# Sparse attention on one core: attention values with the values as the stationary operand, probabilities scaled before they are transposed, three branches added up in PSUM

## The chip, the cores and the metric

The kernel runs on one core of one Trainium2 chip. The metric is the device time of one execution in microseconds (us); the numbers below are medians of several runs, and the trace is one further execution, taken by the hardware profiler. The engines are called as the profile calls them: PE (TensorE, with PEld for its weight loads), DVE (VectorE), ACT (ScalarE), POOL (GpSimd) and SP (SyncE, which issues most DMAs).

## The reference

The program is a stack of thirteen residual layers on 256 tokens of width 1024: seven feed-forward layers, a gated recurrence, a forgetting attention, a short convolution, shared keys and values, and last a sparse attention followed by one more feed-forward layer. The change is in the sparse attention alone. With 16 heads in 4 groups, 256 tokens and every 64-token block selected, it is

```python
p_c = masked_softmax(s_c, rel_c >= 0)                      # 15 compressed keys
o_c = jnp.einsum('bghqn,bgnd->bghqd', p_c, v_c)
p_s = masked_softmax(s_s, (rel_s >= 0)[:, :, None])        # selected blocks
o_s = jnp.einsum('bghqk,bgqkd->bghqd', p_s, v_sel)
p_w = masked_softmax(s_w, mask_w)                          # window
o_w = jnp.einsum('bghqk,bgkd->bghqd', p_w, v_wb)
return gblk[..., 0:1] * o_c + gblk[..., 1:2] * o_s + gblk[..., 2:3] * o_w
...
return out @ w_o
```

## The kernel before

Everything stays on the core; the weights stream in from HBM, 1 MB at a time. A weight piece is split by ACT into a high part `wh` (L177) and by DVE or POOL into a low part `wl` (L179), and each product of the big layers is three matmuls of a 128x128 stationary tile with 256 columns. The order on every engine is the order in which the code emits instructions; there is no scheduler. `tick()` may emit one such split at the points where it is called, paced by a running cost `self.t`. Inside the sparse attention all low parts go to POOL (`pool_parts`).

The sparse attention (`nsa`) works on eight pairs of heads, c = 0 to 7, one after the other. Queries are in halves: token tile 0 sees 128 keys (`p0`), token tile 1 sees 256 (`p1`), each for two branches `br` (selected, window) and two heads `h`. One turn of the loop, in emission order:

- `probs(c)`: PE transposes the twelve 128x128 tiles of p (L250), ACT and DVE copy them out to `pT`, DVE makes r = gate / sum (L1224, L1226).
- `outputs(c - 1)`: PE transposes the finished output `oc` of the pair before (two tiles), ACT rounds it to `zh`, DVE makes the rest `zl`.
- `scores(c + 1)`: PE makes the scores of the next pair, `kT<-qT`, with the two heads on the two halves of TensorE's rows; DVE adds the bias and takes the row minimum (L1191, L1201), ACT takes the exponential and the row sum (L1193, L1203, each followed by the read of the accumulator).
- `values(c)`: twelve products with `pT` stationary and 64 columns of `vv` moving, then eight DVE instructions that scale by r and add into `oc` (L1248). `cmp_values` has put the compressed branch into `oc` beforehand.
- `fill(n)`: n pieces of other work for PE, twelve matmuls each: the later query projections, then the output projection of the pairs already done, each piece followed by one DVE addition into x.

`p1` and `p0` have one buffer each: the reduce for pair c + 1 overwrites the tiles that `probs(c)` has transposed. The value products use one PSUM bank (`O`), scores and transposes share five (`R`).

Of the kernel before, what the change touches and what calls it, by code (L numbers as in the profile page):

```python
# [8 lines left out]
F32 = mybir.dt.float32  # L9
# [4 lines left out]
ALU = mybir.AluOpType  # L14
# [104 lines left out]
class Builder:  # L119
# [979 lines left out]
    def nsa(self, nxt):  # L1099
        nc, tc = self.nc, self.tc  # L1100
        xs = self.xs
        P, B = self.P, self.comp(self.P)
        A, R, O = P[:2], B + [P[2]], P[3:]
        self.ring_at[tuple(P)] = 2
        with tc.tile_pool(name="nsa", bufs=1, reuse_waits="tile") as pl:
            qT = pl.tile([128, 8, 256], F32, name="qT", tag="qT")
            pc = pl.tile([128, 2, 8, 32], F32, name="pc", tag="pc")
            pcT = pl.tile([128, 2, 256], F32, name="pcT", tag="pcT")
            oc = pl.tile([128, 8, 2, 128], F32, name="oc", tag="oc")
            gt = pl.tile([128, 2, 48], F32, name="gt", tag="gt")  # L1110
            qg = pl.tile([128, 1], F32, name="qg", tag="qg")
            nc.gpsimd.memset(pc, 0.0)
# [1 line left out]
            bts, ps, pTs, zs, qs, late = {}, {}, {}, {}, [], []  # L1114
# [50 lines left out]
                    nc.scalar.copy(pcT[:, j], b[:, 0:256])  # L1165
                self.tick()

            def cmp_values(gp):
                for j in range(2):
                    b = self.bank(R)  # L1170
                    for i in range(2):
                        self.mm(b[:, 256 * i:256 * i + 256], pcT[:, j, 128 * i:128 * i + 128], self.vcz[:, gp], cost=432.0)
                    c = 4 * gp + 2 * j
                    nc.scalar.copy(oc[:, c:c + 2].rearrange("p c i d -> p i c d"), b.rearrange("p (i c d) -> p i c d", i=2, c=2))
                self.tick()

            def scores(c):

                gp, bt = c // 4, bts[c]
                p1 = pl.tile([128, 2, 2, 256], F32, name="p1", tag="p1")  # L1180
                p0 = pl.tile([128, 2, 2, 128], F32, name="p0", tag="p0")
                mx = pl.tile([128, 2, 2, 2], F32, name="mx", tag="mx", bufs=2)
                sm = pl.tile([128, 2, 2, 2], F32, name="sm", tag="sm", bufs=2)

                rows = [slice(64 * h, 64 * h + 64) for h in range(2)]
                s1 = [self.bank(R), self.bank(R)]
                for h in range(2):
                    self.mm(s1[h], qT[rows[h], c, 128:256], self.kT[rows[h], gp].rearrange("p r s -> p (r s)"), cost=429.0)
                for h in range(2):
                    for br in range(2):  # L1190
                        nc.vector.tensor_tensor_reduce(  # L1191
                            p1[:, br, h], s1[h][:, 256 * br:256 * br + 256], bt[:, h], 1.0, 3e38, ALU.add, ALU.min, mx[:, 1, br, h:h + 1])
                        nc.scalar.activation(  # L1193
                            p1[:, br, h], p1[:, br, h], AF.Exp, bias=mx[:, 1, br, h:h + 1], scale=-1.0, accum_out=sm[:, 1, br, h:h + 1])
                    self.tick()
                s0 = [self.bank(R), self.bank(R)]
                for h in range(2):
                    self.mm(s0[h][:, 0:256], qT[rows[h], c, 0:128], self.kT[rows[h], gp, :, 0:128], cost=216.0)
                for h in range(2):
                    for br in range(2):  # L1200
                        nc.vector.tensor_tensor_reduce(  # L1201
                            p0[:, br, h], s0[h][:, 128 * br:128 * br + 128], bt[:, h, 128:256], 1.0, 3e38, ALU.add, ALU.min, mx[:, 0, br, h:h + 1])
                        nc.scalar.activation(  # L1203
                            p0[:, br, h], p0[:, br, h], AF.Exp, bias=mx[:, 0, br, h:h + 1], scale=-1.0, accum_out=sm[:, 0, br, h:h + 1])
                self.tick()
                if c + 2 < 8:
                    bias(c + 2)
                ps[c] = (p1, p0, sm)

            def probs(c):  # L1210
                p1, p0, sm = ps.pop(c)
                r = pl.tile([128, 2, 2, 2], F32, name="r", tag="r", bufs=2)
                pT = pl.tile([128, 2, 2, 384], F32, name="pT", tag="pT")
                for br in range(2):
                    for h in range(2):
                        b = self.bank(R)
                        self.transpose(b[:, 128:256], p1[:, br, h, 0:128])
                        self.transpose(b[:, 256:384], p1[:, br, h, 128:256])
                        self.transpose(b[:, 0:128], p0[:, br, h])
                        if h:  # L1220
                            nc.vector.tensor_copy(pT[:, br, h], b[:, 0:384])
                        else:
                            nc.scalar.copy(pT[:, br, h], b[:, 0:384])
                nc.vector.reciprocal(r, sm)  # L1224
                gg = gt.rearrange("p i (h r) -> p i r h", r=3)[:, :, 1:3, 2 * c:2 * c + 2]
                nc.vector.tensor_tensor(r, r, gg, op=ALU.mult)  # L1226
                self.tick()
                pTs[c] = (pT, r)

            def values(c):  # L1230
                gp = c // 4
                pT, r = pTs.pop(c)
                o = self.bank(O)
                for i in range(2):
                    for br in range(2):
                        for h in range(2):
                            at = 256 * i + 128 * br + 64 * h
                            d = slice(64 * (2 * gp + h), 64 * (2 * gp + h) + 64)
                            for kt in range(i + 1):
                                s = pT[:, br, h, 128 * (i + kt):128 * (i + kt) + 128]  # L1240
                                self.mm(o[:, at:at + 64], s, self.vv[:, kt, br, d], kt == 0, kt == i, cost=214.0)
                        self.tick()
                for br in range(2):
                    for i in range(2):
                        for h in range(2):
                            at = 256 * i + 128 * br + 64 * h
                            on = oc[:, c, i, 64 * h:64 * h + 64]
                            nc.vector.scalar_tensor_tensor(on, o[:, at:at + 64], r[:, i, br, h:h + 1], on, op0=ALU.mult, op1=ALU.add)  # L1248

            def outputs(c):  # L1250
                if c % 2 == 0:
                    zs[c // 2] = (
                        pl.tile([128, 2, 256], F32R, name="zh", tag="zh", bufs=2),
                        pl.tile([128, 2, 256], F32R, name="zl", tag="zl", bufs=2),
                    )
                zh, zl = zs[c // 2]
                b = self.bank(O)
                for i in range(2):
                    self.transpose(b[:, 128 * i:128 * i + 128], oc[:, c, i])
                nc.scalar.copy(zh[:, c % 2], b[:, 0:256])  # L1260
                nc.vector.tensor_tensor(zl[:, c % 2], b[:, 0:256], zh[:, c % 2].bitcast(F32), op=ALU.subtract)

            def stream():

# [44 lines left out]
            def fill(n):  # L1309
                for _ in range(n):  # L1310
                    next(main, None)
# [4 lines left out]
            query(1)  # L1316
            cmp_scores(0)
            scores(0)
            fill(3)
            for c in range(8):  # L1320
                probs(c)
                if c:
                    outputs(c - 1)
                if c == 0:
                    g = self.nat_heads_in_two(pl, late[:1], ("qa",), pool=True)
                    q = next(g)
                if c % 4 == 0:
                    cmp_turn(c // 4)
                if c == 3:
                    query(2)  # L1330
                    query(3)
                if c < 7:
                    scores(c + 1)
                    if c == 3:
                        cmp_scores(1)
                    if c % 4 == 0:
                        cmp_values(c // 4)
                    if c == 1:
                        for _ in g:
                            pass  # L1340
                        qs += q
                    values(c)
                    fill((1, 0, 2, 2, 2, 2, 2)[c])
                    if c == 0:
                        for _ in g:
                            pass
                        qs += q
                    if c == 0:
                        g = self.nat_heads_in_two(pl, late[1:], ("qb",), pool=True)
                        q = next(g)  # L1350
            fill(1)
            values(7)
            fill(1)
            outputs(7)
            fill(4)
            self.P = B

    def run(self):
# [209 lines left out]
```

## Time and profile before

| what | value |
|---|---|
| median of 3 runs (lowest to highest) | 2142.56 us (2142.15 to 2143.3) |
| profiled execution: time / span from first to last instruction | 2140.52 us / 2138.4 us |
| mean granted TensorE clock of the profiled execution | 0.994 |
| busy share PE / DVE / ACT / POOL | 98% / 66% / 48% / 19% |
| the sparse attention's loop over pairs, in the trace | 1858.86 to 1944.2 us |

A busy time of PE counts pipelined matmuls whose ends are modelled, so 98% says that PE seldom stands still, not that it runs at its peak. The granted clock is 1.0 at the upper level (2.4 GHz) and 0.5 at the lower (1.2 GHz). The time of a run lies about 2 us above the span.

### The profile page before, as it was taken

How to read it: one execution, taken by the hardware profiler on the slowest of the kernel's cores; microseconds unless marked ns; L12 is line 12 of the kernel's file. 1: busy time of each engine (PE TensorE's matmuls, PEld its weight loads, DVE VectorE, ACT ScalarE, POOL GpSimd, SP SyncE). 2: the span in 40 equal slices, each digit the busy share in tenths (PEclk: the TensorE clock that was granted, in tenths of full speed). 3: DMA queues.
4: the chain of work that ended last, by engine and by line, in shares of the span. 5: the costliest groups of instructions: out<-in, count | busy, mean ns of one | idle time of the engine just before them, and what ended most of it. 6: DMA issues, size and time to landing. Idle time of an engine off the chain costs nothing.

```text
span 2138.4 us, 41531 instructions
## 1 busy us (share of the span) xinstructions
PE 2087.5 (98%) x17299; PEld 2064.0 (97%) x17299; DVE 1419.4 (66%) x2566; ACT 1027.9 (48%) x2076; POOL 401.4 (19%) x357
## 2 busy tenths in 40 slices
PE   8999889999999998999999999999999999999999
PEld 7999889999999998999999999999999999879999
DVE  7656776756666578575667657775578665687554
ACT  5544434544444456654454445454445444565442
POOL 2002646300100023320010001110021100442000
PEclk9999999999999999999999999999999999999999
DMA  7554423595455545345545554555546554223551
GB/s 264 199 191 149 158 80 122 181 238 196 152 205 190 175 158 183 133 175 200 178 158 207 188 179 156 200 193 181 186 174 228 179 185 170 97 101 131 211 190 60
DMA packets 57020, 368.93 MB, mean 173 GB/s; under 512 B 6318, under 2 KB 10694, under 8 KB 14080
## 3 DMA queue, kind: packets, MB, share of 16 engines
q1 hardware_dynamic: 53600, 355.49, 46.3%
q0 software_dynamic: 2656, 10.07, 2.5%
q8 instruction: 135, 2.21, 0.4%
q10 hardware_dynamic: 576, 0.72, 0.1%
q14 instruction: 53, 0.43, 0.1%
HBM read 360.75 MB, written 4.46 MB: 171 GB/s over the span
## 4 chain that ended last, share of the span: by engine, by line
PE 72%; DVE 6%; ACT 2%; issue 1%; POOL 0%; DMA 0%; DVEq 0%; ACTq 0%
PE b L245 71%; DVE wl L179 2%; PE b L250 1%; DVE xl L360 1%; ACT wh L177 1%; DVE x L392 1%; DVE rs_t L423 0%; DVE rs_t L424 0%; ACT xh L356 0%; POOL ssum L372 0%; DMA cd<-cn 0%; DVE nss L675 0%; DVE nrs L425 0%; DVE oc L1248 0%; ACT p L1193 0%
## 5 line engine op out<-in xcount | busy, mean ns | idle before, releaser
L179 DVE TENSOR_TENSOR wl<-wr,wh 128x512 fp32r<-128x512 f32 x1229 | 851.1, 751 | 247.5 <-ACT wh L177 247.3
L245 PE MATMUL b<-xh,wh 128*128 128x256 f32 x3184 | 908.3, 285 | 7.3 <-ACT wh L1430 7.3
L245 PE MATMUL b<-xh,wl 128*128 128x256 f32 x3184 | 904.9, 284 | 2.7 <-DVE wl L1431 2.7
L245 PE MATMUL b<-xl,wh 128*128 128x256 f32 x3184 | 904.4, 284 | 0.0
L177 ACT CAST wh<-wr 128x512 fp32r<-128x512 f32 x1332 | 725.3, 616 | 149.7 <-issue 132.1
L245 PEld LDWEIGHTS b<-xh,wh 128*128 128x128 f32 x3184 | 613.8, 193 | 7.5 <-ACT wh L1430 7.3
L245 PEld LDWEIGHTS b<-xh,wl 128*128 128x128 f32 x3184 | 613.5, 193 | 3.6 <-DVE wl L1431 3.6
L245 PEld LDWEIGHTS b<-xl,wh 128*128 128x128 f32 x3184 | 613.7, 193 | 0.0
L245 PE MATMUL b<-ah,wh 128*128 128x256 f32 x1408 | 394.5, 280 | 0.0
L245 PE MATMUL b<-al,wh 128*128 128x256 f32 x1408 | 394.4, 280 | 0.0
L245 PE MATMUL b<-ah,wl 128*128 128x256 f32 x1408 | 394.2, 280 | 0.0
L480 POOL TENSOR_TENSOR sg<-sg,rb 128x512 f32<-128x512 f32 x88 | 114.2, 1298 | 1245.5 <-ACT sg L479 1245.4
L245 PEld LDWEIGHTS b<-al,wh 128*128 128x128 f32 x1408 | 265.2, 188 | 0.2 <-DVE al L488 0.2
L245 PEld LDWEIGHTS b<-ah,wh 128*128 128x128 f32 x1408 | 265.2, 188 | 0.0
L245 PEld LDWEIGHTS b<-ah,wl 128*128 128x128 f32 x1408 | 264.8, 188 | 0.0
L479 ACT ACTIVATE sg<-g 128x512 f32<-128x512 f32 x88 | 55.6, 632 | 319.9 <-DVE g L477 319.9
L487 ACT CAST ah<-av 128x512 fp32r<-128x512 f32 x88 | 54.6, 621 | 259.6 <-DVE av L484 259.6
L179 POOL TENSOR_TENSOR wl<-wr,wh 128x512 fp32r<-128x512 f32 x103 | 144.2, 1412 | 163.1 <-ACT wh L177 138.7
L477 DVE TENSOR_TENSOR g<-b,rb 128x512 f32<-128x512 f32 x88 | 60.7, 690 | 170.9 <-PE b L245 169.0
L245 PE MATMUL b<-wh,xh 128*128 128x256 f32 x512 | 151.7, 296 | 5.4 <-DVE qn L686 5.4
L245 PE MATMUL b<-wl,xh 128*128 128x256 f32 x512 | 146.3, 286 | 0.0
L245 PE MATMUL b<-wh,xl 128*128 128x256 f32 x512 | 146.1, 285 | 0.0
(256 smaller groups left out, 1919.7 us busy)
## 6 DMA issues: line engine op xcount, KB each, us to landing
wr<-in_W_dram SPq DMA_DIRECT2D x332, 1024.0 KB, 4.8
td<-t POOLq DMA_DIRECT2D x1, 3072.0 KB, 37.5
wr<-in_W_dram SPq DMA_DIRECT2D x8, 256.0 KB, 6.2
bc<-cd POOLq DMA_DIRECT2D x4, 512.0 KB, 4.1
w<-in_CW_dram POOLq DMA_DIRECT2D x2, 1024.0 KB, 13.3
bt<-td SPq DMA_DIRECT2D x8, 256.0 KB, 4.3
x<-in_XT_dram SPq DMA_DIRECT2D x4, 256.0 KB, 5.7
wr<-in_W_dram SPq DMA_DIRECT2D x2, 512.0 KB, 3.8
```

The source lines that it names most:

```text
L177: nc.scalar.copy(h[:, s], r[:, s])
L179: eng.tensor_tensor(l[:, s], r[:, s], h[:, s].bitcast(F32), op=ALU.subtract)
L245: self.nc.tensor.matmul(out, lhsT, rhs, start=start, stop=stop, skip_group_check=True)
L250: self.nc.tensor.transpose(out, in_, self.c("ID")[:n, :n])
L360: self.nc.vector.scalar_tensor_tensor(xs[1][:, d], self.x[:, d], g, xs[0][:, d].bitcast(F32), op0=ALU.mult, op1=ALU.subtract)
L392: nc.vector.scalar_tensor_tensor(x, acc[i], factor, x, op0=ALU.mult, op1=ALU.add)
L477: nc.vector.tensor_tensor(g1, banks[0].rearrange("p (c t) -> p c t", c=2), self.rb2(), op=ALU.mult)
L479: nc.scalar.activation(sg, g1, AF.Silu)
L480: nc.gpsimd.tensor_tensor(sg, sg, self.rb2(), op=ALU.mult)
L487: nc.scalar.copy(ah, av)
```

## The change

The scaling by gate / sum moves from the outputs of the value products to the probabilities: `scale(c)` multiplies `p1` and `p0` in place, on DVE, after the scores of pair c and ahead of `probs(c)`. With the scale inside the probabilities, the three branches can be added in PSUM: the compressed branch starts the sum (`vcz` stationary, `pcT` moving, 256 columns), and eight products follow with `vv` stationary (64 columns of TensorE, head 0 in its lower half, head 1 in its upper) and `pT` moving (256 or 128 columns). The result comes out with features on the partitions, as the output projection wants it, so `oc`, `cmp_values` and `outputs` with its two transposes go; `zh` and `zl` are made straight from the bank.

```diff
+            def scale(c):
+                p1, p0, sm = ps[c]
+                r = pl.tile([128, 2, 2, 2], F32, name="r", tag="r", bufs=2)
+                nc.vector.reciprocal(r, sm)
+                gg = gt.rearrange("p i (h r) -> p i r h", r=3)[:, :, 1:3, 2 * c:2 * c + 2]
+                nc.vector.tensor_tensor(r, r, gg, op=ALU.mult)
+                for i, p, n in ((1, p1, 256), (0, p0, 128)):
+                    pp = p.rearrange("p r h s -> p (r h) s")
+                    rr = r[:, i].rearrange("p r h -> p (r h)")
+                    nc.vector.tensor_tensor(pp, pp, rr[:, :, None].to_broadcast([128, 4, n]), op=ALU.mult)
...
             def values(c):
                 gp = c // 4
-                pT, r = pTs.pop(c)
-                o = self.bank(O)
-                for i in range(2):
-                    for br in range(2):
+                pT = pTs.pop(c)
+                o = self.bank(O)[:, 0:256]
+                self.mm(o, self.vcz[:, gp, 128 * (c % 2):128 * (c % 2) + 128], pcT[:, c % 4 // 2], True, False, cost=432.0)
+                for br in range(2):
+                    for kt in range(2):
                         for h in range(2):
                             d = slice(64 * (2 * gp + h), 64 * (2 * gp + h) + 64)
...
+                            s = pT[:, br, h, 256:384] if kt else pT[:, br, h, 0:256]
+                            self.mm(o[64 * h:64 * h + 64, 128 * kt:256], self.vv[:, kt, br, d], s, False, br == kt == 1, cost=162.0)
...
+                nc.scalar.copy(zh[:, c % 2], o)
+                nc.vector.tensor_tensor(zl[:, c % 2], o, zh[:, c % 2].bitcast(F32), op=ALU.subtract)
...
             scores(0)
+            scale(0)
             fill(3)
             for c in range(8):
                 probs(c)
-                if c:
-                    outputs(c - 1)
...
-                    if c % 4 == 0:
-                        cmp_values(c // 4)
...
                     values(c)
+                    scale(c + 1)
                     fill((1, 0, 2, 2, 2, 2, 2)[c])
...
             fill(1)
             values(7)
-            fill(1)
-            outputs(7)
-            fill(4)
+            fill(5)
```

Three places in the order of the instructions. First DVE, in the turn c = 4, from the end of the reduces (rows named ISA, of which the `mx` rows are the reads of the minimum) to the copies of the next turn. Before:

```order
L1201 ISA p_21931,mx<-b_21947,bt 128x128
L1201 ISA mx 128x1
L1248 SCALAR_TENSOR_TENSOR oc<-b_21968,r,oc 128x64 x8
L1296 TENSOR_TENSOR x<-b_21989,x 128x512
L1296 TENSOR_TENSOR x<-b_22003,x 128x512
L1221 COPY pT<-b_22028 128x384
L1221 COPY pT<-b_22033 128x384
L1224 RECIPROCAL r<-sm 128x8
L1226 TENSOR_TENSOR r<-r,gt 128x8
L1261 TENSOR_TENSOR zl<-b_22047,zh 128x256
```

And of the change, at the same place:

```order
L1191 ISA p_21868,mx<-b_21886,bt 128x128
L1191 ISA mx 128x1
L1249 TENSOR_TENSOR zl<-b_21899,zh 128x256
L1204 RECIPROCAL r<-sm 128x8
L1206 TENSOR_TENSOR r<-r,gt 128x8
L1210 TENSOR_TENSOR p_21867<-p_21867,r 128x1024
L1210 TENSOR_TENSOR p_21868<-p_21868,r 128x512
L1284 TENSOR_TENSOR x<-b_21920,x 128x512
L1284 TENSOR_TENSOR x<-b_21934,x 128x512
L1222 COPY pT<-b_21958 128x384
L1222 COPY pT<-b_21968 128x384
```

The eight scaling additions are gone, and `zl`, the reciprocal, r and two multiplications of p now stand between the reduces of pair 5 and the copies of its transposes.

Second ACT, from the exponentials of pair 5 to the copies of its transposes (L177 are the weight casts). Before:

```order
L1193 ACTIVATE p_21930,sm<-p_21930,mx 128x256 x4
L1203 ACTIVATE p_21931,sm<-p_21931,mx 128x128 x4
L1174 COPY oc<-b_21960 128x2x2x128
L1174 COPY oc<-b_21964 128x2x2x128
L177 CAST wh<-wr 128x512
L1223 COPY pT<-b_22023 128x384
```

And of the change:

```order
L1183 ACTIVATE p_21867,sm<-p_21867,mx 128x256 x2
L1193 ACTIVATE p_21868,sm<-p_21868,mx 128x128 x4
L177 CAST wh<-wr 128x512
L1248 CAST zh<-b_21899 128x256
L177 CAST wh<-wr 128x512
L1224 COPY pT<-b_21953 128x384
```

The rounding to `zh` now follows the exponentials of the next pair, with a weight cast ahead of it and one behind.

Third PE, from the transposes of pair 5 to the first matmuls of the fill. Of the change (before, one row `vv,pT 128x64 x12` stood where the five value rows stand):

```order
L250 MATMUL b_21968<-consts,p_21867 128x128 x2
L250 MATMUL b_21968<-consts,p_21868 128x128
L245 MATMUL b_21977<-kT,qT 128x512
L245 MATMUL b_21978<-kT,qT 128x512
L245 MATMUL b_21993<-kT,qT 128x256
L245 MATMUL b_21994<-kT,qT 128x256
L245 MATMUL b_22005<-pcT,vcz 128x256
L245 MATMUL b_22005<-pT,vv 64x256 x2
L245 MATMUL b_22005<-pT,vv 64x128 x2
L245 MATMUL b_22005<-pT,vv 64x256 x2
L245 MATMUL b_22005<-pT,vv 64x128 x2
L245 MATMUL b_22024<-zh,wh 128x256
```

The transposes are followed by the scores without the two of `oc` between them, and the value products are nine.

## Rows read from the trace of the kernel before

**Rows 1.** The page: busy time of each engine, share, instructions.

```profile
PE 2087.5 (98%) x17299; PEld 2064.0 (97%) x17299; DVE 1419.4 (66%) x2566; ACT 1027.9 (48%) x2076; POOL 401.4 (19%) x357
```

**Rows 2.** Timeline of PE: start, us, engine, line, operation, count [idle before].

```profile
1906.08 1.10 PE L245 MATMUL b<-vcz,pcT 128*128 128x256 f32 x4 [0.16 <-DVE mx L1191]
...
1912.58 1.47 PE L250 MATMUL b<-consts,p 128*128 128x128 f32 x12
1913.88 0.38 PE L250 MATMUL b<-consts,oc 128*128 128x128 f32 x2
1914.20 1.56 PE L245 MATMUL b<-kT,qT 64*128 64x512 f32 x8
1915.69 2.89 PE L245 MATMUL b<-vv,pT 128*128 128x64 f32 x24
1918.39 0.36 PE L245 MATMUL b<-zh,wh 128*128 128x256 f32 x1
...
1921.35 1.47 PE L250 MATMUL b<-consts,p 128*128 128x128 f32 x12
```

**Rows 3.** Timeline of PE: the scores of the other pairs.

```profile
1861.70 1.97 PE L245 MATMUL b<-kT,qT 64*128 64x512 f32 x8
...
1871.97 1.13 PE L245 MATMUL b<-kT,qT 64*128 64x512 f32 x4
...
1879.40 1.56 PE L245 MATMUL b<-kT,qT 64*128 64x512 f32 x8
...
1889.52 1.56 PE L245 MATMUL b<-kT,qT 64*128 64x512 f32 x8 [0.34 <-ACT qT L1125]
...
1903.30 1.56 PE L245 MATMUL b<-kT,qT 64*128 64x512 f32 x8 [0.78 <-DVE pT L1221]
...
1922.96 1.56 PE L245 MATMUL b<-kT,qT 64*128 64x512 f32 x8
...
1944.19 0.28 PE L245 MATMUL b<-zh,wl 128*128 128x256 f32 x1
```

**Rows 4.** Timeline of ACT: last accumulator read of pairs 0 and 6, `zh`, casts.

```profile
1859.69 0.19 ACT L1203 ACTIVATION_READ_ACCUMULATOR p<-p,mx 128x1 f32 x1
...
1914.30 0.37 ACT L1260 CAST zh<-b 128x256 fp32r<-128x256 f32 x1
...
1919.84 0.19 ACT L1203 ACTIVATION_READ_ACCUMULATOR p<-p,mx 128x1 f32 x1
1919.93 1.13 ACT L177 CAST wh<-wr 128x512 fp32r<-128x512 f32 x2
```

**Rows 5.** Timeline of DVE: first reduce of pair 4, one `zl`.

```profile
1890.68 0.42 DVE L1191 CUSTOM_DVE_ANT_0 p<-b,bt 128x256 f32<-128x256 f32 x1 [1.01 <-PE b L245]
...
1914.87 0.42 DVE L1261 TENSOR_TENSOR zl<-b,zh 128x256 fp32r<-128x256 f32 x1
```

**Rows 6.** Single lines on DVE: count, duration in ns (min/median/max), first and last start, shape.

```profile
L765 DVE TENSOR_TENSOR bc<-bc,consts x4: 1211/1216/1220, 815.3 to 872.2; 128x1024 f32<-128x1024 f32 x4
L488 DVE TENSOR_TENSOR al<-av,ah x88: 691/695/696, 36.4 to 2124.5; 128x512 fp32r<-128x512 f32 x88
```

**Rows 7.** Timeline of DVE and POOL: one small DVE multiplication at two moments.

```profile
1855.20 0.18 DVE L1155 TENSOR_TENSOR csm<-csm,consts 128x16 f32<-128x16 f32 x1
...
1897.30 1.21 DVE L1155 TENSOR_TENSOR csm<-csm,consts 128x16 f32<-128x16 f32 x1
...
1895.93 3.78 POOL L179 TENSOR_TENSOR wl<-wr,wh 128x512 fp32r<-128x512 f32 x3 [1.77 <-ACT wh L177]
```

**Rows 8.** Busy time of PE, PEld, DVE, ACT, POOL in stretches; granted clock, DMA share, GB/s.

```profile
214.00:220.00 6.00, 3.08 (x27) 2.88 (x26) 4.67 (x13) 1.46 (x2) 2.00 (x2) 1.00 0.90 335
...
1844.50:1847.90 3.40, 1.34 (x9) 0.89 (x9) 2.35 (x3) 0.79 (x2) 1.03 (x1) 1.00 0.00 0
...
1848.00:1854.80 6.80, 6.80 (x27) 5.06 (x28) 2.31 (x9) 2.73 (x5) 1.27 (x1) 0.50 0.41 154
...
1898.46:1904.00 5.54, 3.04 (x24) 2.33 (x24) 5.47 (x17) 2.40 (x6) 1.62 (x3) 1.00 0.14 46
```

More of the change, by code (lines that the diff above doesn't have):

```diff
@@ L1108, in nsa @@
             pcT = pl.tile([128, 2, 256], F32, name="pcT", tag="pcT")
-            oc = pl.tile([128, 8, 2, 128], F32, name="oc", tag="oc")
             gt = pl.tile([128, 2, 48], F32, name="gt", tag="gt")
@@ L1166, in cmp_turn @@
                 self.tick()
-            def cmp_values(gp):
-                for j in range(2):
-                    b = self.bank(R)
-                    for i in range(2):
[L1172 to L1175, printed above, removed]
             def scores(c):
@@ L1208, in scores @@
                 ps[c] = (p1, p0, sm)
+            def scale(c):
[8 more added lines that the diff above has]
+                    nc.vector.tensor_tensor(pp, pp, rr[:, :, None].to_broadcast([128, 4, n]), op=ALU.mult)
             def probs(c):
                 p1, p0, sm = ps.pop(c)
-                r = pl.tile([128, 2, 2, 2], F32, name="r", tag="r", bufs=2)
                 pT = pl.tile([128, 2, 2, 384], F32, name="pT", tag="pT")
@@ L1223, in probs @@
                             nc.scalar.copy(pT[:, br, h], b[:, 0:384])
-                nc.vector.reciprocal(r, sm)
-                gg = gt.rearrange("p i (h r) -> p i r h", r=3)[:, :, 1:3, 2 * c:2 * c + 2]
-                nc.vector.tensor_tensor(r, r, gg, op=ALU.mult)
                 self.tick()
-                pTs[c] = (pT, r)
+                pTs[c] = pT
             def values(c):
                 gp = c // 4
-                pT, r = pTs.pop(c)
-                o = self.bank(O)
-                for i in range(2):
-                    for br in range(2):
+                pT = pTs.pop(c)
[3 more added lines that the diff above has]
+                    for kt in range(2):
                         for h in range(2):
-                            at = 256 * i + 128 * br + 64 * h
                             d = slice(64 * (2 * gp + h), 64 * (2 * gp + h) + 64)
[L1239 to L1250, printed above, removed]
+                            s = pT[:, br, h, 256:384] if kt else pT[:, br, h, 0:256]
+                            self.mm(o[64 * h:64 * h + 64, 128 * kt:256], self.vv[:, kt, br, d], s, False, br == kt == 1, cost=162.0)
+                    self.tick()
                 if c % 2 == 0:
@@ L1256, in outputs @@
                 zh, zl = zs[c // 2]
[L1257 to L1261, printed above, removed]
+                nc.scalar.copy(zh[:, c % 2], o)
+                nc.vector.tensor_tensor(zl[:, c % 2], o, zh[:, c % 2].bitcast(F32), op=ALU.subtract)
             def stream():
```

## The prediction

> **What bounds the kernel now.** I read the page first: PE is busy for 98% of the span and DVE for 66% [rows 1], so as a whole the kernel is bound by PE, and what shortens PE's work shortens the time, wherever PE does not wait. So the second view was PE's timeline inside the sparse attention. One turn in full swing (c = 5) runs from the transposes at 1912.58 to those at 1921.35, 8.77 us: twelve transposes 1.30, the two of the old output 0.32, the scores 1.49, the values 2.70, two pieces of fill 2.96 [rows 2]. These add up to 8.77: PE waits for nothing. The third view was ACT's timeline, because the transposes need exponentials: the last accumulator read of pair 6 ends at 1920.03 [rows 4], and PE comes to that pair's transposes at 1921.35 [rows 2]. So between "p is ready" and "PE wants it" lie only 1.3 us. The change puts new work into exactly this gap.
>
> I measure a turn from one start of the scores, S(c), to the next. S(1) to S(7) are 1861.70, 1871.97, 1879.40, 1889.52, 1903.30, 1914.20, 1922.96, and the last fill ends the stage at about 1944.3 [rows 2, 3].
>
> **The change, part by part.**
>
> *PE's own work.* Gone per pair: the values' 2.70, the transposes' 0.32, and a product with `vcz` (four records for two of them 1.10, so 0.55 at most). New: that product with 256 columns, 0.5, and eight with half of TensorE's columns. The rows have no matmul with 64 stationary columns. Nearest is `kT`, where the heads lie on the halves of the rows: 1536 columns in 1.49 us [rows 2], while a full product takes 0.5 for 256. One after another these would take 3.0, so halves run side by side there. The new eight have 2 x (2 x 256 + 2 x 128) = 1536 columns too: 1.3 to 1.5 if halves of columns do the same, 2.6 to 3.0 if not. I take 1.3, so values 1.8 and a turn of 1.30 + 1.49 + 1.8 + 2.96 = 7.55. Saved: 1.7 per pair, 13.3 over eight, if PE were what the turn waits for.
>
> *The path through the scaling.* It is not. From S(6) at 1914.20 to the last exponential's read at 1920.03 are 5.83 us, with one weight cast in the middle; without it 5.3 [rows 2, 4]. A DVE with less to do doesn't shorten this: the first reduce starts 1.16 after the scores even where DVE sat idle before it [rows 3, 5]. Behind the exponentials now come, by the order in front: on ACT a weight cast 0.52 and `zh` 0.37 [rows 4]; on DVE `zl` 0.42 [rows 5], which stands ahead of the scaling and needs that `zh`; the reciprocal and r, some 0.2 each (a small multiplication takes 0.18 [rows 7]); the multiplication of p1, 1024 elements, 1.21, and of p0, 512 elements, 0.69 [rows 6]. Together 3.6. The first two transposes can start when p1 is done, the third needs p0, and ten are left behind it: 10 x 0.108 = 1.08. So a turn lasts 5.83 + 3.6 + 1.08 = 10.5 us where PE has 7.55 of work. PE stands idle for about 3 us ahead of the transposes, and all that PE saves goes into this wait. What DVE no longer does (eight additions) was behind PE's values and held up nobody in such a turn.
>
> By turns, with this chain:
> - First transposes: the exponentials of pair 0 end at 1859.88 [rows 4]; 0.4 + 1.21 + 0.69 and 1.08 behind them give 1863.3, with the compressed branch's transposes S(1) at 1863.7: +2.0.
> - S(1) to S(2): chain 5.3 + 3.6 + 1.08 = 10.0, and 0.4 because the norm of the later queries holds DVE, against 10.27: +0.1.
> - S(2) to S(3): 10.0 against 7.43, no fill here: +2.6.
> - S(3) to S(4): 10.5 and 1.2 for the query transposes (eight by 0.108 and 0.34 of waiting [rows 3]), against 10.12: +1.6.
> - S(4) to S(5): before 13.78. DVE's softmax of the compressed branch stands ahead of the scaling; its last small step ends at 1898.5 [rows 7], two more and `zl`, r, p1, p0 take 3.2, transposes 1.6: 1903.3 to 1904.3 against 1903.30. I take +0.5.
> - S(5) to S(6): 10.5 against 10.90: -0.4.
> - S(6) to S(7): 10.5 against 8.76: +1.75.
> - S(7) to the end: 5.83 + 3.1 (no cast ahead of `zh`) + 1.08, then 1.48 + 1.8 + 5 x 1.48, is 20.7 against 21.35: -0.65.
>
> Sum: **+7.5 us**.
>
> *DVE and POOL.* A DVE multiplication with both inputs in SBUF took 0.18 us while POOL was idle and 1.21 while POOL worked through three low parts of 1.26 each [rows 7]: it waited out one of them. The scaling is of this kind, and the casts around `zh` send low parts to POOL just then. With two behind one another (pairs 3, 5 and 6) p1 finds the second and waits 1.3; pair 0 about 1.3 for p0, pair 7 about 1.0, pairs 1 and 2 0.3 each: 6.8 in all if POOL always comes first, 0 if DVE does. The row with three in a chain is the nearest, so I take 5. The Trainium skill says the same of this pair of engines ("SBUF — State Buffer", Who interferes with whom): a DVE instruction with two SBUF inputs contends with GpSimd's reads, and the one that comes first blocks the other for its whole length. By it alone the term would be anything up to 6.8, by separate ports nothing; the trace agrees, with 1.21 against 0.18.
>
> *The granted clock.* PE will stand still for 3 to 5 us once in each of eight turns. In the trace a stretch in which PE was busy for 1.34 of 3.40 us was followed by 6.8 us at 0.50, the lower level of 1.2 GHz; one with 3.08 of 6.00 and one with 3.04 of 5.54 kept the upper [rows 8]. Which of them the new turns, with their wait in one piece, resemble more, these rows don't decide. A fall that lasts half as long as the one shown loses 1.7 us of work; part of it falls on transposes and scores (on the path), part on values and fill (eaten up by the next wait). Bounds 0 and 8 x 1.7 = 13.6; I take six falls of 1 us: 6.
>
> The sum is 7.5 + 5 + 6 = 18.5 us. The profiled execution took 2140.52, so 2159; the median of the runs shown lies 2.0 above it, so 2161, and I round to **2160 us**.
>
> **Rivals.**
> - *The path holds, but the clock stays up and DVE mostly wins against POOL*: 2142.6 + 7.5 = 2150. For it: two of the three stretches shown kept the clock. 17%.
> - *Both charges in full*: 7.5 + 6.8 + 13.6 = 28, so 2170. Waits made longer by POOL invite the falls. 20%.
> - *The halves of columns don't run side by side*, so the change doesn't do what it says: each turn has 1.3 us more of PE work, which lies in the wait; only the last pair pays, +1.3, and shorter waits give fewer falls: 2157 to 2161. Against it: the `kT` rows. It is no time of its own, so its one chance in five is in the others.
> - *PE's saving counts (faster)*: the scaling would have to be ready when PE reaches the transposes, 1.49 + 1.8 + 2.96 = 6.25 us after S; the exponentials alone end at 5.83, so the price of the scaling at which the sign turns is about 0.4 us for no wait at all and 1.85 for a turn as long as before. The rows say 3.6. If it happened, 13.3 us would go: 2129. 4%. The Trainium skill ("TensorEngine Tiling (Array Packing)", When to Use Tiling) recommends just this swap for a moving side of 64 columns, at up to twice the speed; no run here shows it yet, and it speaks of TensorE alone, not of who waits for it.
> - *Within the noise*: DVE multiplies p at twice the speed of [rows 6] and the clock holds; each turn is then about 1 us shorter and 0 to 3 us are left: 2144. 6%.
>
> **How the numbers follow.** The forecast (chain, and part of both charges, 2153 to 2167) has 53%. The range runs from 2148, just below the chain alone, to 2171, just above both charges in full; it leaves out the two last rivals and the outer part of the second and of the first, together about 2 in 10. A change of 0.2%, 4.3 us, is about what a measurement of this kernel tells from none: faster 0.04, same 0.06, slower 0.90.
>
> **What would show it.** In the new profile's PE timeline each group of `consts,p` transposes should have a wait of 2.5 to 5 us ahead of it, released by DVE's multiplication of p (L1210), and a second of about 0.5 before the third transpose. S(6) to S(7) should be 10.5 to 12 us with PE busy for about 7.5 of it. The nine products should take 1.8 us (3.1 if halves don't overlap). p1's multiplication should last 1.2 us alone and up to 2.5 beside POOL's L179. The granted clock should show stretches of 0.5 between 1862 and 1955. The prediction is wrong if those transposes follow the fill without a wait, or if S to S is below 9 us.

## The result, and the profile after

The changed kernel takes **2169.71 us** (median; 2142.78 for the kernel before in the same job), ratio 1.0124 [1.0104, 1.0144]: slower by 27 us, where 2160 was forecast. One of its four executions took 2868 us at a mean granted clock of 0.65 and is left out of the ratio. The time lies inside the range, but above the 2153 to 2167 that I gave the best chance and at the 2170 of the rival "both charges in full". The profiled span is 2167.9 us against 2138.4, so +29.5.

The page, busy time of each engine:

```profile
PE 2091.0 (96%) x17219; PEld 2059.2 (95%) x17219; DVE 1425.2 (66%) x2519; ACT 1026.9 (47%) x2072; POOL 402.6 (19%) x356
```

PE has 80 instructions fewer than before [rows 1] and yet 3.5 us more busy time: some of its work now runs at the lower clock. The timeline of PE in the loop over pairs, start, duration, count, and [idle before <- releaser]; `kT,qT` is S(c) for c = 1 to 7:

```profile
1868.09 1.56 PE L245 MATMUL b<-kT,qT 64*128 64x512 f32 x8
1876.82 0.41 PE L250 MATMUL b<-consts,p 128*128 128x128 f32 x2 [3.46 <-DVE p L1210]
...
1879.02 2.81 PE L245 MATMUL b<-kT,qT 64*128 64x512 f32 x8
1888.55 2.97 PE L250 MATMUL b<-consts,p 128*128 128x128 f32 x12 [4.65 <-DVE p L1210]
1891.45 1.72 PE L245 MATMUL b<-kT,qT 64*128 64x512 f32 x8
...
1906.34 1.56 PE L245 MATMUL b<-kT,qT 64*128 64x512 f32 x8 [0.33 <-ACT qT L1124]
...
1922.62 1.56 PE L245 MATMUL b<-kT,qT 64*128 64x512 f32 x8
1932.75 2.97 PE L250 MATMUL b<-consts,p 128*128 128x128 f32 x12 [3.42 <-DVE p L1210]
1935.65 1.80 PE L245 MATMUL b<-kT,qT 64*128 64x512 f32 x8
1937.39 0.70 PE L245 MATMUL b<-pcT,vcz 128*128 128x256 f32 x2
1938.02 1.52 PE L245 MATMUL b<-pT,vv 128*64 128x256 f32 x16
...
1946.03 0.41 PE L250 MATMUL b<-consts,p 128*128 128x128 f32 x2 [3.44 <-DVE p L1210]
1946.63 2.37 PE L250 MATMUL b<-consts,p 128*128 128x128 f32 x10 [0.19 <-DVE p L1210]
1948.93 1.99 PE L245 MATMUL b<-kT,qT 64*128 64x512 f32 x8
```

Each group of transposes has a wait ahead of it that the multiplication of p ends; before, no group had one ahead of it ([rows 2] shows two of the eight). S(6) to S(7) went from 8.76 to 13.28 us. Against [rows 2, 3], S(1) comes 6.4 us later, the six turns to S(7) are longer by 0.7, 5.0, 4.8, 2.5, 2.1 and 4.5, and the rest of the span by 3.5: together the 29.5. Of this, 3.3 lie outside the sparse attention: its compressed scores already start 2.0 later (1849.88 against 1847.85), ahead of everything that the change touches, and 1.3 is a wait of PE in the layer behind it. The start of the compressed scores varies like this between the traces of this case (1846.8 to 1850.4). From there to the first matmul of the next layer the kernel before takes 96.5 us and the changed one 122.7: 26.2 more, near the 27 of the runs. Below I call this the stage. The waits, us in total, times, longest:

```profile
PE b L250 <- DVE p L1210: 29.2, 13, 4.6
```

Inside the turn from S(6) to S(7), the end of the exponentials on ACT, and what DVE and POOL then do:

```profile
1941.54 0.19 ACT L1193 ACTIVATION_READ_ACCUMULATOR p<-p,mx 128x1 f32 x1
1941.63 0.60 ACT L177 CAST wh<-wr 128x512 fp32r<-128x512 f32 x1
1942.14 0.36 ACT L1248 CAST zh<-b 128x256 fp32r<-128x256 f32 x1
```

```profile
1942.54 0.42 DVE L1249 TENSOR_TENSOR zl<-b,zh 128x256 fp32r<-128x256 f32 x1 [3.17 <-ACT zh L1248]
1942.88 0.19 DVE L1204 RECIPROCAL r<-sm 128x8 f32<-128x8 f32 x1
1943.11 0.50 DVE L1206 TENSOR_TENSOR r<-r,gt 128x8 f32<-128x8 f32 x1
1943.64 2.85 DVE L1210 TENSOR_TENSOR p<-p,r 128x1024 f32<-128x1024 f32 x2
```

```profile
1942.31 2.49 POOL L179 TENSOR_TENSOR wl<-wr,wh 128x512 fp32r<-128x512 f32 x2 [1.76 <-ACT wh L177]
```

DVE stands idle for 3.17 us, then does `zl`, r and p in a row, while POOL makes two low parts. The groups of the scaling on DVE, x count | busy us, mean ns | idle before:

```profile
L1210 DVE TENSOR_TENSOR p<-p,r 128x1024 f32<-128x1024 f32 x8 | 13.8, 1726 | 0.3
L1210 DVE TENSOR_TENSOR p<-p,r 128x512 f32<-128x512 f32 x8 | 6.5, 815 | 0.0
L1206 DVE TENSOR_TENSOR r<-r,gt 128x8 f32<-128x8 f32 x8 | 3.0, 376 | 0.3
```

Stretches of the same turns, columns as in [rows 8] (the granted clock is the third number from the right):

```profile
1929.00:1932.80 3.80, 0.38 (x4) 0.20 (x4) 3.47 (x5) 0.74 (x2) 2.49 (x2) 1.00 0.13 20
1932.80:1936.20 3.40, 3.40 (x14) 2.70 (x16) 2.61 (x5) 0.96 (x2) 0.00 (x0) 0.50 0.71 289
1936.20:1946.40 10.20, 6.76 (x52) 4.79 (x48) 6.22 (x22) 5.43 (x20) 3.78 (x3) 1.00 0.00 0
1946.40:1949.80 3.40, 3.21 (x13) 2.50 (x14) 2.40 (x5) 0.96 (x2) 0.00 (x0) 0.50 0.00 0
...
1858.00:1978.00 120.00, 90.35 (x605) 72.03 (x605) 78.69 (x227) 62.77 (x202) 39.46 (x51) 0.89 0.18 58
```

and the last of these for the kernel before:

```profile
1858.00:1978.00 120.00, 114.53 (x901) 103.97 (x900) 93.07 (x308) 79.58 (x230) 42.54 (x54) 1.00 0.31 107
```

The clock falls to 0.50 once behind each of these waits, mostly over transposes and scores (in pair 7, over the last transposes and the fill). Before it stayed at 1.00 for these 120 us; now the mean is 0.89, which makes about 2 x 0.11 x 120 = 26 us at the lower level; a stretch like the two shown, 3.4 us each, stands behind each of the eight pairs' waits, 27 us together.

### The profile page after: what moved, and what is told of

Read it like the earlier page. It is cut to its first block, busy times and chain, and to the rows that moved or that the text cites. A ratio compares the mean times of both kernels' runs of the same rounds, so it can differ in the third digit from the quotient of the medians.

```text
span 2167.9 us, 41299 instructions
## 1 busy us (share of the span) xinstructions
PE 2091.0 (96%) x17219; PEld 2059.2 (95%) x17219; DVE 1425.2 (66%) x2519; ACT 1026.9 (47%) x2072; POOL 402.6 (19%) x356
## 4 chain that ended last, share of the span: by engine, by line
PE 70%; DVE 8%; ACT 3%; issue 1%; DMA 0%; POOL 0%; DVEq 0%; ACTq 0%
PE b L245 69%; DVE wl L179 2%; PE b L250 2%; DVE xl L360 1%; DVE p L1210 1%; ACT p L1183 1%; ACT wh L177 1%; DVE x L392 1%; ACT p L1193 1%; DVE rs_t L423 0%; DVE rs_t L424 0%; DMA cd<-cn 0%; ACT xh L356 0%; DVE nrs L425 0%; DVE nss L675 0%
## 5 line engine op out<-in xcount | busy, mean ns | idle before, releaser
L177 ACT CAST wh<-wr 128x512 fp32r<-128x512 f32 x1332 | 726.0, 617 | 150.6 <-issue 132.2
## 6 DMA issues: line engine op xcount, KB each, us to landing
w<-in_CW_dram POOLq DMA_DIRECT2D x2, 1024.0 KB, 12.9
```

The source lines that it names most:

```text
L177: nc.scalar.copy(h[:, s], r[:, s])
```

## The experiments

The theory: p has to be multiplied between the exponentials and the transposes, DVE is slowed by POOL while it does so, and the clock falls behind the wait. Rivals: PE's own work sets the turn after all; one of the two charges is not there; VectorE's work as such is the bound. Each run was timed beside the kernel before, which took 2141.65 to 2142.85 us. The interval of each ratio reaches 2 to 3 us to either side, so a difference between two runs is known to a few us only.

**r in PSUM** (takes POOL's contention away). The unused half of the O bank holds r:

```diff
-                r = pl.tile([128, 2, 2, 2], F32, name="r", tag="r", bufs=2)
+                r = ob[:, 256 + 8 * (c % 2):264 + 8 * (c % 2)].rearrange("p (i r h) -> p i r h", i=2, r=2)
...
-                o = self.bank(O)[:, 0:256]
+                o = ob[:, 0:256]
...
+            ob = self.bank(O)
```

> The scale r is written to and read from the unused half of the O bank in PSUM, so each multiplication of p has one input in SBUF and one in PSUM. Theory (the path through the scaling, lengthened by POOL's port and by the clock): p1 takes 1.2 us and p0 0.7 in every turn instead of 1.73 and 0.82 on the mean, r some 0.2 instead of 0.38; that is 6.7 us over eight turns, and the clock falls stay, so about 2163 us. Rival (POOL's overlap hides in waits that are there anyway): 2168 to 2170, with the same shorter multiplications.

Measured 2160.07, ratio 1.0088 [1.0073, 1.0103], 9.6 below the changed kernel. With one input in PSUM the groups of L1210 are

```profile
L1210 DVE TENSOR_TENSOR p<-p,b 128x1024 f32<-128x1024 f32 x8 | 9.8, 1220 | 0.3
L1210 DVE TENSOR_TENSOR p<-p,b 128x512 f32<-128x512 f32 x8 | 5.4, 680 | 0.0
```

so p1 and p0 lose 13.8 + 6.5 - 9.8 - 5.4 = 5.1 us, and r, which takes 174 ns here, 1.6 more: 6.7 of contention. The other 3 us fit the clock, whose falls I had expected to stay: its mean over the 120 us is 0.91, and the stretches at the lower clock add up to 20.5 us, two falls of 3.4 fewer.

```profile
1858.00:1978.00 120.00, 94.66 (x672) 75.51 (x671) 79.84 (x242) 65.67 (x205) 38.68 (x51) 0.91 0.23 77
```

**Spare matmuls in the wait** (takes the clock's falls away). Twenty matmuls whose result nobody reads, ahead of each `probs(c)`:

```diff
+            dm = pl.tile([128, 256], F32R, name="dm", tag="dm")
+            nc.scalar.copy(dm, self.vv[:, 0, 0])
...
             for c in range(8):
+                w = self.bank(R)
+                for _ in range(20):
+                    self.mm(w[:, 0:256], dm[:, 0:128], dm)
                 probs(c)
```

> Twenty matmuls of 256 columns on spare data stand ahead of each pair's transposes, 2.4 us of PE work inside waits of 2.2 to 4.7 us; their result goes to a spare bank and is not used. Theory: PE seldom stands still, the eight stretches at 0.50 in the loop go, and with them 8 x 1.0 to 1.7 us on the transposes and scores: 2156 to 2161 us. Rival (the slow stretches are eaten up by the waits behind them): 2168 to 2171 with the clock at 1.00.

Measured 2159.79, 1.0088 [1.0073, 1.0103]. One fall is left where there were eight, p1 is as slow as in the changed kernel (1739 ns), and PE still waits for it behind the spare work:

```profile
1858.00:1978.00 120.00, 106.83 (x827) 89.83 (x826) 86.07 (x242) 65.24 (x204) 40.46 (x51) 0.99 0.23 77
```

```profile
1935.40 2.55 PE L245 MATMUL b<-dm 128*128 128x256 f32 x20
1939.04 0.41 PE L250 MATMUL b<-consts,p 128*128 128x128 f32 x2 [1.09 <-DVE p L1210]
```

Seven falls fewer are 9.9 us by the times, 1.4 each. By the stage in the traces (113.9 against 122.7) they are 8.7 us, 1.25 each.

**No multiplication of p.** The condition is never true, so the two multiplications are left out; r is still made:

```diff
-                    nc.vector.tensor_tensor(pp, pp, rr[:, :, None].to_broadcast([128, 4, n]), op=ALU.mult)
+                    if c < 0:
+                        nc.vector.tensor_tensor(pp, pp, rr[:, :, None].to_broadcast([128, 4, n]), op=ALU.mult)
```

> The two multiplications of p by the scale are left out, all else is as in the change, so the attention's branches are added without their weights. Theory: without these 1.9 us (2.5 with POOL's share) the transposes wait for exponentials, zl and r no longer; PE has work for 7.6 us a turn and the exponentials end 5.8 us after the scores, so PE waits little, the clock stays up and the saving of PE shows: 2130 to 2136 us. Rival (the products with half of the columns or their place cost time themselves): above 2143.

Measured 2134.45, 0.9967 [0.9955, 0.998]. The transposes now follow the fill (twelve in 1.47, no wait), and the clock falls twice:

```profile
1916.38 1.47 PE L250 MATMUL b<-consts,p 128*128 128x128 f32 x12
```

So PE's saving is there, but in this order only if p need not be multiplied on the way: some 35 us lie between this run and the changed kernel. It is not yet free of waits: PE stands 4.0 us for DVE's copies of `pT`.

**Scale first**: `scale(c + 1)` emitted ahead of `values(c)`, so neither `zh` nor `zl` stands before it.

```diff
                     scores(c + 1)
+                    scale(c + 1)
...
                     values(c)
-                    scale(c + 1)
```

> scale(c + 1) is emitted ahead of values(c), so on DVE the reciprocal, r and the multiplications of p come ahead of zl, and no longer wait for ACT's weight cast and zh. Theory: the path behind the exponentials is 1.3 us shorter in each of seven turns (0.52 + 0.37 + 0.42), some of it lost to POOL in another place: 2155 to 2161 us, the wait ahead of the transposes 1 us shorter. Rival (the clock alone makes the wait dear, so a shorter wait with the same falls gains less than half of that): 2163 to 2168.

Measured 2159.27, 1.0084 [1.0069, 1.0099]. PE's waits for p go from 29.2 to 18.2 us, but POOL's low part now meets p0 instead of p1,

```profile
L1210 DVE TENSOR_TENSOR p<-p,r 128x512 f32<-128x512 f32 x8 | 14.1, 1760 | 0.0
L1210 DVE TENSOR_TENSOR p<-p,r 128x1024 f32<-128x1024 f32 x8 | 9.8, 1225 | 0.3
```

and the third transpose waits for it (1.26 in most turns). In the turn from S(4) the compressed branch's softmax has moved behind the scaling, and PE waits 3.14 and 0.72 for that. Some 24 us, seven falls of 3.4, are still at the lower clock (mean 0.90).

**Scale first and r in PSUM; the same with ten spare matmuls; scores two pairs ahead with r in PSUM.** The edits are those of the first, the second and the fourth run together, and for the third that of the last pair of runs below with r in the O bank. Three misses with one cause.

> Two of the prices taken off together: the scaling ahead of zl, and r in PSUM. Theory (prices of chain, POOL and clock that add up): behind the exponentials stand 0.4 + 1.21 + 0.69 = 2.3 us, a turn of scores takes 5.8 + 2.3 + 1.08 = 9.2 us against 8.8 of the kernel before, the wait ahead of the transposes is 1.5 us and only some turns still lower the clock (2 to 4 falls of 1.4): 2143 to 2150 us. Rival (something else in the change costs, so that it stays above whatever is taken off the path): 2152 to 2158.

> As the one before, with ten matmuls on spare data (1.2 us) ahead of each pair's transposes, so that the clock stays up. Theory: what is left is the chain alone, 9.2 us a turn, some turns cheaper than in the kernel before: 2140 to 2146 us, no stretch at 0.50 in the loop. Rival as above: over 2150.

> The scores run two pairs ahead instead of one (p1 and p0 in two buffers, in the room that oc left), r in PSUM: in turn c the scores of pair c + 2, then the scaling of pair c + 1, whose exponentials were taken a turn earlier. Theory: the path through the scaling no longer ends a turn; PE has work for 7.6 us and DVE for about 7.7 (copies 1.1, reduces 2.3, scaling 2.4, zl 0.4, two additions 1.4), so a turn takes 7.7 to 8.2 instead of 8.8, the first turn somewhat longer: 2132 to 2140 us, faster than both kernels, no falls after pair 1. Rival (DVE's queue, now with all of it in one row, holds the copies of the next transposes): 2142 to 2150.

Measured 2189.18 (1.0218 [1.0203, 1.0234]), 2193.84 (1.024 [1.0225, 1.0256]) and 2170.97 (1.0137 [1.012, 1.0153]). The first one's PE:

```profile
1927.78 1.47 PE L250 MATMUL b<-consts,p 128*128 128x128 f32 x12
...
1937.80 1.22 PE L245 MATMUL b<-pcT,vcz 128*128 128x256 f32 x2 [6.62 <-DVE p L1210]
```

Most transposes don't wait any more (2.4 us are left), but the values do, seven times and 43.4 us in all. r shares its tile with the sum of the values, and with the scaling ahead of `values(c)` the product with `vcz` waits until DVE has read r. The spare matmuls of the second run leave this wait as it is (43.9 us in all), and the third run has it too, 4.15 us in most turns. My edit made this wait; the runs say nothing on the order itself.

**Halves apart**: the eight value products first all for one half of the columns, then for the other.

```diff
-                for br in range(2):
-                    for kt in range(2):
-                        for h in range(2):
+                for h in range(2):
+                    for br in range(2):
+                        for kt in range(2):
```

> The change with the eight products in another order: all four of head 0 (lower half of the columns), then all four of head 1. Theory 1 (halves run side by side only where neighbours lie on different halves): the eight products take 2.3 to 2.7 us instead of 1.5, all of it inside the waits ahead of the transposes, so the time stays within 3 us of the change, 2166 to 2171, with less wait; it may fall by a few us if shorter waits lower the clock less often. Theory 2 (a product with half of the columns is simply quicker): 1.5 us as before. Rival on the time (PE's work counts): 8 us more.

Measured 2169.33, 1.0126 [1.0111, 1.0141], the time of the changed kernel.

```profile
1937.93 2.22 PE L245 MATMUL b<-pT,vv 128*64 128x256 f32 x16
1945.96 0.41 PE L250 MATMUL b<-consts,p 128*128 128x128 f32 x2 [2.74 <-DVE p L1210]
```

The products take 0.70 longer and the wait behind them is 0.70 shorter; in all, PE's waits for p go from 29.2 to 24.2 us: PE's own work is off the path. Neighbouring products on the two halves overlap, neighbours on one half overlap less.

**Scale first in eight pieces**: one multiplication per half, branch and head, by a column of r, p1's ahead of r for p0; the compressed branch's softmax is split around the scaling.

```diff
...
-                    nc.vector.tensor_tensor(pp, pp, rr[:, :, None].to_broadcast([128, 4, n]), op=ALU.mult)
...
+                    for br in range(2):
+                        for h in range(2):
+                            nc.vector.tensor_scalar(p[:, br, h], p[:, br, h], r[:, i, br, h:h + 1], None, op0=ALU.mult)
```

> The scaling cut into eight multiplications by a scalar of each row (one input and the scalar, 0.35 us for 256 elements and about 0.22 for 128 by the rows of such instructions), p1's four as soon as its four sums are there, while ACT still takes the exponentials of p0; all of it ahead of zl; the compressed branch's softmax in two parts around the scaling of pair 4. Theory: behind the last exponential stand 0.4 + 0.9 us and the last transposes, 1.5 to 2.3 us instead of 4.7, so a turn of scores takes 7.6 to 8.2 us and the saving of PE shows at last: 2131 to 2139 us, no or few falls of the clock. Rival (POOL holds the port against these too, up to 1.3 us in a turn): 2140 to 2148.

Measured 2149.9, 1.0039 [1.0026, 1.0051]: a miss, above the theory's range and 2 us above that of its rival, which has the mechanism. The waits for p shrink to 12.9 us and the clock's mean is 0.96; POOL still comes between (the 128x128 pieces, which meet it more often, take longer on the mean than the larger ones: 0.2 us alone and up to 1.3 beside it):

```profile
L1211 DVE TENSOR_SCALAR p<-p,r 128x128 f32<-128x128 f32 x32 | 17.3, 603 | 0.3
L1211 DVE TENSOR_SCALAR p<-p,r 128x256 f32<-128x256 f32 x32 | 11.2, 413 | 0.3
```

**Scale first with ten spare matmuls**:

> The scaling ahead of zl as in the run before that did this alone (2159.3), and ten matmuls on spare data ahead of each pair's transposes (1.2 us, inside waits of 1.7 to 2.9). Theory (a fall of the clock costs 1.4 us): five to seven of that run's seven stretches of 3.4 us at 0.50 go: 2149 to 2153 us. Rival (the spare matmuls lie on the path here, since the waits are short): 2156 to 2162.

Measured 2160.87, 1.0086 [1.0071, 1.0102]: a miss, in the range of its rival. The spare work stands in PE's order ahead of the transposes, and where they follow it without a wait it can only have delayed them. The clock still falls behind waits that come later, five falls' worth instead of seven, with a mean of 0.93 (0.90 without the spare work):

```profile
1911.66 1.35 PE L245 MATMUL b<-dm 128*128 128x256 f32 x10
1912.85 1.56 PE L250 MATMUL b<-consts,p 128*128 128x128 f32 x12
1917.15 0.30 PE L250 MATMUL b<-consts,pc 128*128 128x128 f32 x1 [2.74 <-DVE pc L1157]
```

In the traces the stage is 1.7 us shorter than without the spare work, in the times nothing is gained; a difference of this size is below what these runs can tell.

**Two pairs ahead, r in a tile of its own**, p1 and p0 with two buffers each; the later queries one turn earlier; and the same with the scaling of pair c + 1 ahead of the scores of pair c + 2. Of the first:

```diff
-                if c == 3:
+                if c == 0:
+                    scores(1)
+                if c == 2:
...
+                if c < 6:
+                    scores(c + 2)
                 if c < 7:
-                    scores(c + 1)
+                    if c:
+                        scale(c + 1)
...
                     values(c)
-                    scale(c + 1)
+                    if c == 0:
+                        scale(1)
```

> The same order as the run with the scores two pairs ahead, but r stands in a buffer of its own in SBUF, so the O bank has one user. Theory (the time lies in the wait ahead of the transposes and in the clock that falls after it, and the 4.2 us wait ahead of the values in the earlier run came from the shared bank): the waits ahead of the values go, the transposes of the pairs from 2 on keep no wait over 0.7 us although the multiplication of p1 by itself goes back to 1.7 us beside GpSimd, at most two clock falls are left in the loop, and the time is 2131 to 2140 us. Rival 1 (the two-ahead order itself costs, because PE now has no work between a pair's scores and its values): turns stay at 13 us and the time is 2160 or more. Rival 2 (VectorE's work as such is the bound of the turn, wherever it stands): 2145 to 2155 us.

> As the other run of this call, with the scaling of pair c + 1 ahead of the scores of pair c + 2 instead of behind them: VectorE multiplies while TensorE transposes, and the first reduction of pair c + 2 comes some 2 to 3 us later. Theory: no wait of TensorE for the scaling is left at all from pair 2 on, and since nothing in this turn waits for the exponentials of pair c + 2, the later reductions cost nothing: 2130 to 2138 us, and not slower than the other run. Rival (the scores hold their PSUM banks longer, and the next transposes or projections wait for a bank): a new wait on reductions ahead of the kT products or transposes of 1 to 2 us a turn, 2142 to 2152 us.

Measured 2145.71 (1.0018 [1.0009, 1.0027]) and 2148.4 (1.003 [1.0018, 1.0042]): 24 and 21 us better than the changed kernel, but above the ranges I gave. The first one's PE:

```profile
1861.14 0.41 PE L250 MATMUL b<-consts,p 128*128 128x128 f32 x2 [1.75 <-DVE p L1210]
1862.81 1.97 PE L250 MATMUL b<-consts,p 128*128 128x128 f32 x10 [1.26 <-DVE p L1210]
...
1878.64 2.97 PE L250 MATMUL b<-consts,p 128*128 128x128 f32 x12 [4.99 <-DVE p L1210]
...
1897.20 1.47 PE L250 MATMUL b<-consts,p 128*128 128x128 f32 x12
...
1910.07 0.30 PE L250 MATMUL b<-consts,pc 128*128 128x128 f32 x1 [1.70 <-DVE pc L1157]
...
1913.24 2.93 PE L245 MATMUL b<-kT,qT 64*128 64x512 f32 x8 [1.09 <-DVE pT L1222]
```

The wait ahead of the values is gone, and from pair 3 on the transposes of p wait for nothing. Of the 9.4 us that PE still waits for p, 8.0 are in pairs 0 and 1, whose scaling I had not moved ahead. In the turn of pair 4 PE waits for DVE three times more, 3.7 us in all, because the compressed branch's softmax stands behind the scaling in DVE's order: 1.70 and 0.87 for `pc`, 1.09 for a copy of `pT`. The three stretches at the lower clock that remain (17 us) lie behind the waits of pairs 0, 1 and 4. The next turn has no wait: from the transposes at 1921.88 to those at 1929.77 are 7.89 us, against 8.77 in the kernel before [rows 2], so there PE's saving shows.

The second run has no wait for p after pair 1 at all, but 2.8 for the compressed branch, 2.1 for DVE's copies of `pT` and 1.8 for ACT's, which the first doesn't have: a new wait took the old one's place, as its rival said, though it stands at the copies and not at the banks. Rival 2 of the first run, VectorE's work as such, has the right time but not the cause: the turn of 7.89 us has all of DVE's work in it, and PE waits only where that work stands in one row ahead of it, in the first pairs and in pair 4. A version with these pairs mended wasn't run, so whether this order can fall below the kernel before is open.

## Why the prediction was right, and where its sizes were off

- **PE's own saving.** The products with halves of columns take 1.5 us for 1536 columns and side by side, as taken from the `kT` rows; the nine take 2.1 (1937.39 to 1939.47) instead of 1.8. That the saving goes into the wait is shown twice: 0.7 us more work leaves the time alone (halves apart), and without the multiplication of p the kernel is faster than before (2134). That last run is the faster rival's mechanism, 2129 by the forecast, with the scaling's price set to nothing. Two pairs ahead, a turn without waits lasts 7.89 us, near the 7.55 of the forecast. The Trainium skill's advice for this swap ("TensorEngine Tiling (Array Packing)", When to Use Tiling), up to twice the speed, agrees with the trace for TensorE's products alone (2.70 us before [rows 2], 1.45 now), and the kernel is slower all the same.
- **The chain behind the exponentials.** Right in every link. From S(6) the last read ends after 6.08 us (forecast 5.83; the scores ran in part at the lower clock). From there to the first transposes 4.30 (2.92): `zh` and `zl` as forecast, r 0.3 more, p1 2.2 instead of 1.21. From there to S(7) 2.90 (1.77), with the transposes at 0.50. Sum 13.28, where I gave 10.5 to 12 for this turn: the excess is the two charges, 1.3 and about 1.4, not the chain. The second wait is 0.19, not 0.5, and 1.26 in pair 0, where POOL meets p0.
- **DVE and POOL.** 6.7 us by the durations, 5 forecast, 6.8 the bound: POOL came first in all seven pairs in which the forecast had them meet. In the trace it meets p0 in pair 0, r and p1 in pairs 3, 5 and 6, p1 in pair 7, and r alone in pairs 1 and 2. One input in PSUM ends it: p1 takes 1726 ns on the mean and up to 2245 in the changed kernel, and 1220 with r in PSUM. The Trainium skill ("SBUF — State Buffer", Who interferes with whom) has a DVE instruction with two inputs in SBUF contend with GpSimd's reads, and one with at most one, outside certain fast modes, not contend. The trace agrees, with 1726 against 1220.
- **The granted clock.** The term that was mis-sized most, inside its bounds. I took six falls of 1 us; there were eight, and each costs 1.25 to 1.4, so 10 to 11. The reason for taking less, that part of a fall lands on values and fill where the next wait absorbs it, didn't hold in most turns: the falls lie behind the wait, over transposes and scores, and twelve transposes take 2.97 there and 1.47 at the upper level [rows 2].
- **What is left for the chain** is 2169.7 - 2142.8 - 6.7 - 11.3 = 9 us, against 7.5. So all three terms were short, by about 1.5, 1.7 and 4 to 5 us. That the time came out at the rival with both charges in full (7.5 + 6.8 + 13.6) is in part luck: its charge for the clock was too dear, and its chain too cheap. The split is a subtraction: the charges feed each other, as the run with r in PSUM shows, which lost two falls as well (6.7 + 2 x 1.4 = 9.5, and 9.6 measured, nearer than these runs can tell).

## What to carry to other kernels

An edit that spares the bound engine work gains only if the engine does not then wait for the work that was moved: find the latest input of the next step, and cost the new link at that place, with what stands ahead of it in each queue. A wait on TensorE can cost more than itself: in the changed kernel the clock fell behind waits of 2.2 to 4.7 us, mostly just where the critical work resumed, for 1.25 to 1.4 us each. To hide a scaling like this one, the most that helped here was to move the whole producer a step ahead with buffers of its own; that came to within 4 us of the kernel before, not below it. A spare corner of a tile that another engine uses made a new wait.

## What was not expected of the hardware

A small multiplication can lose about as much to POOL as a large one. r (128x8) took 174 ns in PSUM, 376 in the changed kernel and, two pairs ahead, 621 on the mean and up to 1001, while p1 there was back at 1225. So moving the scaling moved the contention from p1 to p0 (1760 ns) or to r. Only the last order, with the scaling ahead of the scores, nearly escapes it: r 210, p1 1225 and p0 819 (680 with r in PSUM), 1.4 us in all instead of 6.7, because in most turns POOL has no low part to make while DVE scales. The groups of r in the two runs with pairs two ahead, the last order below:

```profile
L1206 DVE TENSOR_TENSOR r<-r,gt 128x8 f32<-128x8 f32 x8 | 5.0, 621 | 0.3
L1206 DVE TENSOR_TENSOR r<-r,gt 128x8 f32<-128x8 f32 x8 | 1.7, 210 | 0.3
```

Matmuls that nobody reads, placed in a wait that is there anyway, gave back 9 to 10 us; ten of them in an order with shorter waits gave nothing that the times show.
